# One hybrid encoder layer: head scales in one operation, edge columns on ScalarE, a split rotation and a new order of the mixer

## The chip, the cores and the metric

The kernel runs on one core of a Trainium2 chip. A core has five engines that run at the same time, each through its own list of instructions: PE (TensorE, matrix products into PSUM), DVE (VectorE), ACT (ScalarE), POOL (GpSimd) and SP (SyncE, which here only issues transfers). An engine takes its instructions strictly in the order of its list; one that has to wait for another engine or for a transfer holds up everything behind it. The metric is the time of one execution on the device in microseconds (us); smaller is better.

## The reference

One layer works on 512 positions of 1024 features, in single precision:

```python
x = x + 0.5 * swiglu(rms_norm(x, g1), w_gate1, w_up1, w_down1)
u = rms_norm(x, gm) @ w_in          # fourier 512 | q 8x64 | k 2x64 | v 2x64
a = fourier_mixer(u[:, :512])       # real part of a 2-D transform over positions and the
                                    # 128 channels of each of 4 groups, then fnet_w, fnet_b
q, k = rms_norm per head, then the axial rotation:
       [x1*cos - x2*sin, x1*sin + x2*cos] on each half of a head
b = softmax(q @ k.T / 8) @ v        # 8 query heads share 2 key heads
x = x + concat(a, b) @ w_out
x = x + 0.5 * swiglu(rms_norm(x, g2), w_gate2, w_up2, w_down2)
y = rms_norm(x, gf)
```

The feed-forward width is 2752. `rms_norm(x, g)` is x times (mean of squares + 1e-6) to the power -1/2 times g.

## The kernel before, in words

Activations lie transposed in SBUF: features (or head channels) on the 128 partitions, the 512 positions along the row. The program has three parts, one after the other: the first feed-forward block, the mixer (projection, Fourier branch, attention, output projection; roughly 345 to 495 us of the profiled span), and the second feed-forward block with the final norm. Only the mixer is touched here.

**Products in three passes.** PE multiplies in a format that is rounded. To keep single precision, every operand is held as a high part (a rounded copy) and a low part (the value less its high part), and `product` (L171 to L174) runs high by high (L172), high by low (L173) and low by high (L174). So each weight block and each intermediate needs two more operations before PE may use it: the high part, which ACT makes (or DVE for names in `HI_DVE`), and the low part, a subtraction (`lows`, L131) on DVE, or on POOL for names in `LOWS_POOL`. PE's first two passes can begin with the high parts of the weights alone; what each pass waits for is the part it reads.

**Who sets the order.** The mixer is written as some 600 small named steps. Each is recorded by `op(name)`, and the table `ORDER` lists the names in the order in which they are executed; each engine, SP's and POOL's queues of transfers too, gets its instructions in exactly this order. So one step placed earlier in the table is placed ahead of other steps on every engine that it uses.

The names: `wX.r/.h/.l` load a weight block and make its parts (X is k, q0 to q3, v, f0 to f3, fw, o0 to o7). `k.0` to `v.7` are the eight steps of each projection of keys, queries and values. Per query block q0 to q3, and for k, the rotation consists of `.sw` (ACT copies the projection times the gain), `.sd` (SP transfers that swap the halves into a second tile `sw_q`), `.rc` (DVE, times the cosines, into `rot_q`), `.rs` (DVE, L944: `sw_q` times the sines; L945: added to `rot_q`). Then `.ah/.al/.bh/.bl` make high and low parts of the two head sets in `qa` and `qb`. The scale of a head comes from squares (`.sq`, ACT), sums of them on PE (`.pq`), two small DVE operations (`.s0`, L962 and L963), a power on POOL (`.s1`, L968) and a factor on POOL (`.s2`, L972); the factors `rr` and `rq` are made from the norm of the mixer's input in step `n1.p` (L1397, L1398). Keys get their scale through `kw` (a broadcast copy), `kp` (PE transposes it) and `km`; `k0.0` to `k1.3` make their high and low parts in `ks`.

Attention works on 32 items `tbc` (query block t, key head b, block c of 128 queries): `s` (two matmuls of scores, L1230 and L1231), `m` (DVE: scale and row extreme, L1236), `e` (ACT: exponential, L1245), `x` (DVE: a transposition, L1254), `h` and `l` (parts, into `its`). `vr0.*` and `vr1.*` spread the values with transfers on POOL's queue, four each (L1062). `p0` to `p3` multiply probabilities with values; `o*.c/.a`, `z*.r/.w/.p` and `r*.m/.h/.l` add, divide by the sums and split the result. The Fourier branch: `f{h}{c}.0/.1` (PE, L1101), `.u` (ACT) or `.e` (DVE, L1122), `.h/.l`; `map*`; `d{g}0/1` (product over positions) with `.h/.l`; then `c{g}.c` and `c{g}.s` (the products with cosines and sines over the channels), `c{g}.q` (ACT copy), `c{g}.o` (DVE, into the tile `fo`: the two edge columns at L1207, two halves of 255 columns at L1211), `c{g}.h/.l`. The output projection is `y{d}.0` to `y{d}.7` (d is a block of 128 features), then `y{d}.x` (DVE, adds to x, L1337), `.h` (ACT) and `.l` (DVE, L203), which scale and split x for the next block, `.q` (ACT, square, L209) and `.a` (DVE, adds the squares in `acc`, L1350), whose sum gives the next norm (products `ss`, L231).

**Banks.** All products of the mixer share the eight PSUM banks. A step takes the bank that has been free the longest when the table reaches it (`bank_for`), and hands it back after its last reader (`read`). A product can therefore also wait for the engine that reads what was in its bank before.

## Time and profile before

| | |
|---|---|
| median of 3 runs | 833.85 us (832.57, 833.85, 833.99) |
| the profiled execution | 831.53 us |
| its span, first to last instruction | 829.7 us |
| outside the span | 1.8 us |
| mean granted TensorE clock | 0.999 |
| busy: PE, DVE, ACT, POOL | 818.9, 602.6, 458.7, 131.9 us |

The rows follow in the prediction. In rows of the timeline the first number is the start in us from the start of the span, the second the length, then engine, line, operation, what it writes and reads, and in brackets how long the engine was idle before it and who released it. The columns of a row by windows are: the stretch, its length, busy time (and count) of PE, of PE's weight loads, DVE, ACT and POOL, the granted clock, the share of the DMA engines, GB/s. Groups of instructions show engine, operation, out<-in, count, then busy us and mean ns of one, then idle time ahead of them and who ended it.

### The profile page before, as it was taken

How to read it: one execution, taken by the hardware profiler on the slowest of the kernel's cores; microseconds unless marked ns; L12 is line 12 of the kernel's file. 1: busy time of each engine (PE TensorE's matmuls, PEld its weight loads, DVE VectorE, ACT ScalarE, POOL GpSimd, SP SyncE). 2: the span in 40 equal slices, each digit the busy share in tenths (PEclk: the TensorE clock that was granted, in tenths of full speed). 3: DMA queues.
4: the chain of work that ended last, by engine and by line, in shares of the span. 5: the costliest groups of instructions: out<-in, count | busy, mean ns of one | idle time of the engine just before them, and what ended most of it. 6: DMA issues, size and time to landing. Idle time of an engine off the chain costs nothing.

```text
span 829.7 us, 14444 instructions
## 1 busy us (share of the span) xinstructions
PE 818.9 (99%) x5734; PEld 742.5 (89%) x5734; DVE 602.6 (73%) x939; ACT 458.7 (55%) x794; POOL 131.9 (16%) x138
## 2 busy tenths in 40 slices
PE   9999999999999999999989999999999999999997
PEld 6888998899989998889978878899988998899986
DVE  7987884578656857699998578878745884578562
ACT  7664663366434645577887257546623663266452
POOL 0121000000000000259794300200000000000001
PEclk9999999999999999999999999999999999999999
DMA  7787774567374514335350335877463774566122
GB/s 255 190 188 205 185 204 139 112 170 216 89 195 122 152 40 133 127 108 121 100 101 28 97 103 130 214 185 205 134 190 92 193 192 134 127 166 181 45 81 102
DMA packets 50724, 119.33 MB, mean 144 GB/s; under 512 B 5728, under 2 KB 14560, under 8 KB 50528
## 3 DMA queue, kind: packets, MB, share of 16 engines
q1 hardware_dynamic: 38128, 92.57, 34.1%
q0 software_dynamic: 12256, 25.57, 18.7%
q8 instruction: 45, 0.74, 0.4%
q10 hardware_dynamic: 272, 0.26, 0.1%
q14 instruction: 23, 0.19, 0.1%
HBM read 111.83 MB, written 2.10 MB: 137 GB/s over the span
## 4 chain that ended last, share of the span: by engine, by line
PE 95%; DVE 3%; issue 1%; POOLq 0%; POOL 0%; ACT 0%; DVEq 0%
PE r L449 23%; PE q L449 11%; PE dn L173 9%; PE dn L172 9%; PE dn L174 9%; PE p L449 6%; PE mix L172 3%; PE mix L174 3%; PE mix L173 3%; PE gu L787 3%; PE gu L172 2%; PE gu L174 2%; PE gu L173 2%; PE mix L1270 2%; PE mix L1101 1%; PE last L1475 1%
## 5 line engine op out<-in xcount | busy, mean ns | idle before, releaser
L449 PE MATMUL r<-rt,ring 128*128 128x256 f32 x1686 | 204.9, 277 | 0.0
L449 PEld LDWEIGHTS r<-rt,ring 128*128 128x128 f32 x1686 | 198.5, 188 | 0.9
L173 PE MATMUL dn<-at,ring 128*128 128x512 f32 x295 | 114.9, 389 | 0.0
L174 PE MATMUL dn<-at,ring 128*128 128x512 f32 x295 | 114.9, 389 | 0.0
L172 PE MATMUL dn<-at,ring 128*128 128x512 f32 x295 | 114.9, 389 | 0.0
L449 PE MATMUL q<-rt,ring 128*128 128x256 f32 x840 | 106.6, 276 | 0.0
L394 ACT CAST ring<-s 128x1024 fp32r<-128x1024 f32 x70 | 73.4, 1049 | 58.2 <-DVE s L414 51.4
L601 DVE SCALAR_TENSOR_TENSOR gx<-dn,gx 128x512 f32<-128x512 f32 x61 | 42.1, 691 | 80.5 <-PE dn L174 80.5
L449 PEld LDWEIGHTS q<-rt,ring 128*128 128x128 f32 x840 | 100.4, 188 | 0.0
L366 POOL DMA_DIRECT2D s<-in_wgu x35 | 30.1, 860 | 424.3 <-DMA s<-in_wgu 177.5
L131 DVE TENSOR_TENSOR ring<-s,ring 128x1024 fp32r<-128x1024 f32 x70 | 85.3, 1219 | 0.6 <-ACT ring L394 0.6
L164 ACT CAST ring<-raw_dn 128x768 fp32r<-128x768 f32 (+2 forms) x48 | 40.8, 853 | 75.4 <-PE dn L173 70.5
L174 PEld LDWEIGHTS dn<-at,ring 128*128 128x128 f32 x295 | 55.4, 188 | 11.5
L173 PEld LDWEIGHTS dn<-at,ring 128*128 128x128 f32 x295 | 55.4, 188 | 11.0
L172 PEld LDWEIGHTS dn<-at,ring 128*128 128x128 f32 x295 | 55.4, 188 | 11.0
L449 PE MATMUL p<-rt,ring 128*128 128x256 f32 x420 | 53.3, 276 | 0.0
L131 DVE TENSOR_TENSOR ring<-raw_dn,ring 128x768 fp32r<-128x768 f32 (+2 forms) x48 | 46.7, 977 | 7.0 <-ACT ring L164 6.9
L449 PEld LDWEIGHTS p<-rt,ring 128*128 128x128 f32 x420 | 50.2, 188 | 0.0
L131 DVE TENSOR_TENSOR ring<-raw_g,ring 128x1024 fp32r<-128x1024 f32 x36 | 43.8, 1217 | 0.0
L131 DVE TENSOR_TENSOR at<-u,at 128x512 fp32r<-128x512 f32 x35 | 24.2, 693 | 20.2 <-ACT at L504 20.2
L492 DVE TENSOR_TENSOR u<-g,u 128x512 f32<-128x512 f32 x35 | 24.0, 687 | 19.8 <-ACT u L489 19.8
L131 POOL TENSOR_TENSOR its<-x,its 128x512 fp32r<-128x512 f32 x26 | 36.0, 1406 | 7.0 <-ACT its L1256 6.6
(332 smaller groups left out, 1551.7 us busy)
## 6 DMA issues: line engine op xcount, KB each, us to landing
raw_g<-in_wgu SPq DMA_DIRECT2D x36, 512.0 KB, 4.1
s<-in_wgu SPq DMA_DIRECT2D x70, 256.0 KB, 4.3
s<-in_wgu POOLq DMA_DIRECT2D x35, 512.0 KB, 5.7
raw_dn<-in_wd SPq DMA_DIRECT2D x44, 384.0 KB, 4.0
raw_u<-in_wgu SPq DMA_DIRECT2D x35, 256.0 KB, 4.0
raw_gu<-in_wgu SPq DMA_DIRECT2D x11, 512.0 KB, 3.5
raw_o<-in_wo SPq DMA_DIRECT2D x8, 512.0 KB, 3.8
raw_dn<-in_wd SPq DMA_DIRECT2D x5, 448.0 KB, 4.2
```

The lines of the kernel that those rows point to most:

```text
L131: (by or nc.vector).tensor_tensor(out=lo, in0=src, in1=asf(hi), op=ALU.subtract)
L164: nc.scalar.copy(hi[:, :n, :], raw[:, :n, :])
L172: nc.tensor.matmul(ps, whi, mhi, start=first, stop=False)
L173: nc.tensor.matmul(ps, whi, mlo, start=False, stop=False)
L174: nc.tensor.matmul(ps, wlo, mhi, start=False, stop=last)
L366: nc.gpsimd.dma_start(out=blocks(t), in_=up, accum_op=ALU.add)
L394: nc.scalar.copy(ts[0], src)
L449: nc.tensor.matmul(ps[:, c], a[:, ks], b[:, i, c], start=first and i == 0 and o == 0, stop=i == KH - 1 and o == 2, skip_group_check=not fi ...
L492: nc.vector.tensor_tensor(out=self["u"], in0=self["g"], in1=self["u"], op=ALU.mult)
L601: nc.vector.scalar_tensor_tensor(out=x[d][:, t], in0=ps[:, t], scalar=0.5, in1=x[d][:, t], op0=ALU.mult, op1=ALU.add)
L787: nc.tensor.matmul(pss[c], w[:, k % 2, c], m[k], start=k == 0 and m is hh and w is hi, stop=k == KD - 1 and w is lo,)
L1270: nc.tensor.matmul(sets[st][a][:, : 8 * 32], vrep[rows, j], its[rows, o, :, 32 * j : 32 * j + 32], start=j == 0 and o == 0, stop=j == 15 a ...
```

## The change

- **Head scales (`.s0`, `.s1`).** One DVE operation in place of two: sums/64 plus `em`, where `em` is EPS times the input norm's mean of squares. The power on POOL stays, `.s2` and the factors `rr` and `rq` go: the norm of the mixer's input cancels in a normalized head but for its EPS term. The factor -1/8 goes into the gain of the queries (`qkg[:, 0:1]`). Both preparations stand on POOL ahead of the power of the input's norm in `n1.p`.
- **`kw`** is a copy on ACT, before on DVE.
- **Edge columns.** New steps `c{g}.t` on ACT (Identity with a bias) in place of the DVE operation at L1207.
- **The rotation's addition** is a step of its own, `.ra`. For the names in the new table `ADDS_DMA`, which holds q2, it is a transfer on POOL's queue that adds `sw_q` (128 rows of 512) to `rot_q` in place of the DVE operation.
- **`k1.1` and `k1.2`** are transfers on POOL's queue (64 rows of 512) that copy the part that another step made, in place of a DVE subtraction and an ACT copy.
- **Two tables** of who makes which part: 33 names in place of 34 in `LOWS_POOL`; `HI_DVE` has 300, f0, o3, o4, wq3 in place of 203, o3, o6, o7, wq1, wq2.
- **`ORDER`** is new. The number of matmuls stays the same.

```diff
 LOWS_POOL = """
-000 001 003 010 011 012 013 100 101 102 103 110 111 113 200 201 202 203 211 212 213 300 301 303 311 312 f0 fw o0 o1
-o2 o5 o6 o7
+000 002 010 011 012 013 100 101 103 110 111 113 200 201 202 203 212 213 300 301 302 303 310 311 313 f3 o0 o1 o2 o4
+o5 o6 wq3
+ADDS_DMA = """
+q2
 HI_DVE = """
-203 o3 o6 o7 wq1 wq2
+300 f0 o3 o4 wq3
...
 ORDER = """
-wk.r wq0.r wv.r cos wk.h wk.l wq0.h k.0 k.1 k.2 k.3 k.4 wv.h k.5 wq0.l k.6 wq1.r k.7 k.sq q0.0 wq1.h n1.c q0.1 wq3.r
+wk.r wq0.r wv.r cos wk.h wk.l wq0.h k.0 k.1 k.2 k.3 k.4 wv.h k.5 wq0.l k.6 wq1.r k.7 k.sq q0.0 wq1.h n1.c k.pq q0.1
...
             @op(f"{name}.rs")
             def _():
+                sw = swaps[name]
+                nc.vector.tensor_tensor(out=sw, in0=sw, in1=sin, op=ALU.mult)
+
+            @op(f"{name}.ra")
+            def _():
                 r, sw = rots[name], swaps[name]
-                nc.vector.tensor_tensor(out=sw, in0=sw, in1=sin, op=ALU.mult)
-                nc.vector.tensor_tensor(out=r, in0=r, in1=sw, op=ALU.add)
+                if name in ADDS_DMA:
+                    nc.gpsimd.dma_start(out=r, in_=sw, accum_op=ALU.add)
+                else:
+                    nc.vector.tensor_tensor(out=r, in0=r, in1=sw, op=ALU.add)
...
             @op(f"{name}.s0")
             def _():
                 pq = banks[f"pq{name}"][:, 0:8].rearrange("p (c t) -> p c t", t=2)
-                nc.vector.tensor_tensor(out=pq, in0=pq, in1=rr.unsqueeze(2).to_broadcast([P, 4, 2]), op=ALU.mult)
-                nc.vector.tensor_scalar(out=v, in0=pq, scalar1=1.0 / HD, scalar2=EPS, op0=ALU.mult, op1=ALU.add)
+                nc.vector.scalar_tensor_tensor(
+                    out=v, in0=pq, scalar=1.0 / HD, in1=em.unsqueeze(2).to_broadcast([P, 4, 2]), op0=ALU.mult, op1=ALU.add
+                )
                 read(f"pq{name}")
...
-            @op(f"{name}.s2")
-            def _():
-                nc.gpsimd.tensor_tensor(out=v, in0=v, in1=factor.unsqueeze(2).to_broadcast([P, 4, 2]), op=ALU.mult)
...
             @op("kw")
             def _():
-                nc.vector.tensor_copy(kw, sc[0].unsqueeze(3).to_broadcast([P, 4, 2, HD]))
+                nc.scalar.copy(kw, sc[0].unsqueeze(3).to_broadcast([P, 4, 2, HD]))
...
+                if v:
+                    op("k1.1")(lambda own=own, oth=oth, h1=h1, h2=h2: nc.gpsimd.dma_start(out=h1[oth], in_=h2[own]))
+                    op("k1.2")(lambda own=own, oth=oth, h1=h1, h2=h2: nc.gpsimd.dma_start(out=h2[oth], in_=h1[own]))
+                    op("k1.3")(lambda own=own, h1=h1, h2=h2: lows(h2[own], rots["k"][own], h1[own]))
+                    continue
...
+            @op(f"c{g}.t")
+            def _():
+                fos[g, 1] = o = tp.tile([P, S], F32, tag="g", name=f"fo{g}")
+                nc.scalar.activation(
+                    o[:, 0:257:256], banks[f"pc{g}"][:, 0:257:256], AF.Identity, bias=fb[:, g : g + 1]
+                )
...
-                nc.vector.tensor_scalar(
-                    out=o[:, 0:257:256], in0=pc[:, 0:257:256], scalar1=b, scalar2=None, op0=ALU.add
-                )
...
         @op("n1.p")
         def _():
+            nc.gpsimd.tensor_scalar(out=em, in0=n1.ms, scalar1=EPS, scalar2=None, op0=ALU.mult)
+            nc.gpsimd.tensor_scalar(out=qkg[:, 0:1], in0=qkg[:, 0:1], scalar1=-scale, scalar2=None, op0=ALU.mult)
             n1.power(0, 4)
-            nc.gpsimd.tensor_tensor(out=rr, in0=n1.r, in1=n1.r, op=ALU.mult)
-            nc.gpsimd.tensor_scalar(out=rq, in0=n1.r, scalar1=-scale, scalar2=None, op0=ALU.mult)
```

What the new order does is shown at three places. A line number moves by 4 to 16 between the two programs (L131 is L135 after, L1350 is L1366).

The first place is the end of the mixer on DVE, before: `gx<-mix` is `y7.x`, the two operations on `raw_gu` belong to the next block's weights, `ring<-gx` are `y5.l` and `y7.l`, and `acc` with `sq_5`, `sq_7`, `sq_6` are the additions `y5.a`, `y7.a`, `y6.a`.

```order
L1337 TENSOR_TENSOR gx<-mix_3406,gx 128x512
L203 SCALAR_TENSOR_TENSOR ring<-gx,ring 128x512
L1350 TENSOR_TENSOR acc_5277<-acc_5277,sq_5_0_5366 128x512
L131 TENSOR_TENSOR ring<-raw_gu_1_5410,ring 128x1024
L131 TENSOR_TENSOR at_5405<-raw_gu_42_5414,at_5405 128x1024
L203 SCALAR_TENSOR_TENSOR ring<-gx,ring 128x512
L1350 TENSOR_TENSOR acc_5277<-acc_5277,sq_7_0_5381 128x512
L1350 TENSOR_TENSOR acc_5277<-acc_5277,sq_6_0_5384 128x512
```

The same place on DVE after:

```order
L1353 TENSOR_TENSOR gx<-mix_3406,gx 128x512
L207 SCALAR_TENSOR_TENSOR ring<-gx,ring 128x512
L135 TENSOR_TENSOR ring<-raw_gu_1_5399,ring 128x1024
L135 TENSOR_TENSOR at_5394<-raw_gu_42_5403,at_5394 128x1024
L207 SCALAR_TENSOR_TENSOR ring<-gx,ring 128x512
L1366 TENSOR_TENSOR acc_5218<-acc_5218,sq_7_0_5374 128x512
```

The additions of `y5.a` and `y6.a` have moved ahead of `y7.x`.

The second place is the channel stage of the Fourier branch on DVE, before: `oo` is `r1.m`, `el` is `c1.l`, the two L1236 are `m312` and `m212`, then `x313`, `d31.l` (the low part that `c3.s` reads) and `c2.o`.

```order
L1315 TENSOR_TENSOR oo_4188<-mix_3405,oo_4188 128x512
L131 TENSOR_TENSOR el_3423<-fo_4695,eh_3419 128x512
L1236 TENSOR_SCALAR mix_3403,mx_4733<-mix_3403,sc_3438 128x512
L1236 TENSOR_SCALAR mix_3409,mx_4735<-mix_3409,sc_3437 128x512
L1254 STREAM_TRANSPOSE x_4739<-e_4623 128x512
L131 TENSOR_TENSOR ring<-mix_3407,ring 128x255
L1207 TENSOR_SCALAR fo_4751<-mix_3404,fb 128x2
L1211 SCALAR_TENSOR_TENSOR fo_4751<-mix_3404,fb,fq_4723 128x255 x2
```

After, from `c0.l` (`el`) over `c1.o` and `d31.l` (128x255) to `m312`, `m313`, `x212` and `d30.l` (128x257):

```order
L135 TENSOR_TENSOR el_3422<-fo_4604,eh_3418 128x512
L1227 SCALAR_TENSOR_TENSOR fo_4655<-mix_3409,fb,fq_4682 128x255 x2
L135 TENSOR_TENSOR ring<-mix_3408,ring 128x255
L1252 TENSOR_SCALAR mix_3402,mx_4700<-mix_3402,sc_3438 128x512
L1252 TENSOR_SCALAR mix_3407,mx_4710<-mix_3407,sc_3438 128x512
L1270 STREAM_TRANSPOSE x_4721<-e_4693 128x512
L135 TENSOR_TENSOR ring<-mix_3406,ring 128x257
```

`c1.o` and `d31.l` have come ahead of the two `m`, `r1.m` is earlier still, and the last low part in the row is that of `d30`; `c3.s` and `c2.c` on PE stand behind these.

The third place is DVE around the rotation of q2, after: L948 on `sw_q_3704` is `q2.rs`; `rot_q_3815` and `sw_q_3781` are q3's; `qa_3430` is `q2.al`.

```order
L948 TENSOR_TENSOR sw_q_3704<-sw_q_3704,early 128x512
L135 TENSOR_TENSOR ring<-raw_f_3694,ring 128x1024
L940 TENSOR_TENSOR rot_q_3815<-early 128x512
L1252 TENSOR_SCALAR mix_3406,mx_3817<-mix_3406,sc_3436 128x512
L1252 TENSOR_SCALAR mix_3405,mx_3833<-mix_3405,sc_3436 128x512
L135 TENSOR_TENSOR its<-x_3774,its 128x512
L135 TENSOR_TENSOR its<-x_3787,its 128x512
L948 TENSOR_TENSOR sw_q_3781<-sw_q_3781,early 128x512
L973 SCALAR_TENSOR_TENSOR sc_3438<-mix_3404,em 128x8
L1270 STREAM_TRANSPOSE x_3868<-e_3842 128x512
L135 TENSOR_TENSOR qa_3430<-rot_q_3741,qa_3430 64x512
```

Before, the product with the sines and the addition stood together and `q2.al` came six operations later:

```order
L944 TENSOR_TENSOR sw_q_3719<-sw_q_3719,early 128x512
L945 TENSOR_TENSOR rot_q_3778<-rot_q_3778,sw_q_3719 128x512
L1236 TENSOR_SCALAR mix_3408,mx_3811<-mix_3408,sc_3436 128x512
L1254 STREAM_TRANSPOSE x_3815<-e_3767 128x512
L962 TENSOR_TENSOR mix_3402<-mix_3402,rr 128x8
L963 TENSOR_SCALAR sc_3437<-mix_3402 128x8
L936 TENSOR_TENSOR rot_q_3820<-early 128x512
L131 TENSOR_TENSOR qa_3430<-rot_q_3778,qa_3430 64x512
```

The addition of q2 has left DVE; it stands on POOL's queue, after, behind four transfers of values:

```order
L1075 DMA vrep<-its 32x4x128 x4
L954 DMA rot_q_3741<-sw_q_3704 128x512
L135 TENSOR_TENSOR its<-x_3699,its 128x512
L1075 DMA vrep<-its 32x4x128 x4
L980 TENSOR_TENSOR sc_3437<-sc_3437,mhalf 128x8
```

More of the change, by code (lines that the diff above doesn't have):

```diff
@@ L71 @@
-z0.r d00 z0.w o10.c o11.c z1.r h112 d00.h o2.l x113 d01 x110 map0.l m013 d01.h o10.a o11.a d00.l d01.l d10 o1.l h012
-s213 d10.h l112 d11 e013 d10.l m213 h113 s313 x011 s010 h110 c0.s d11.h c0.q h011 s111 vr1.0 m010 vr1.1 d21 l012
-l110 c0.c m313 e010 m111 e313 d20 d11.l d21.h l113 c0.o x010 o4.r d30 d20.h d20.l c0.h d21.l c0.l c1.s c1.c l011
-c2.s h010 vr1.3 z0.p d30.h x013 vr1.2 c1.q e111 o0.r d30.l c2.c s212 c1.o d31 s312 x111 z1.w h013 z1.p c1.h r0.m
-e213 y2.0 c2.q d31.h l010 h111 s311 o0.h l013 c1.l m312 m212 s310 x313 l111 d31.l e212 c3.s y2.1 c2.o r1.m e312 c3.q
@@ new lines @@
+q3.sw q3.sd x003 s100 f2.h q2.rs q3.sq h002 f03.0 vr0.2 h001 e103 f1.l q3.rc m100 f01.0 h003 q2.ra m101 l001 q3.pq
+l003 q3.rs e100 q3.s0 f02.0 h102 q2.ah l002 q2.pq vr0.3 x100 q2.al q2.s0 q2.bh q3.ra f02.1 l102 q2.s1 f00.0 f00.1
+fw.r s203 s202 f2.l q3.s1 q3.ah x103 q3.al f03.1 s200 e101 f3.h f00.u m202 s201 h100 x101 s302 q3.bh z0.r f01.1 m203
+h103 f02.e e202 m200 h101 f3.l m201 e203 s300 x202 m300 f01.u e200 l100 f02.h l103 o1.r e201 z0.w fw.h f03.e x203
+o2.r q3.bl l101 f03.h f11.0 f02.l s303 f11.1 e300 f11.u m302 x200 p0 x300 e302 h200 f03.l s301 pos fw.l h300 f10.0
@@ new lines @@
+e111 c0.t z1.p l013 d10.h d21 r1.m x111 d10.l l113 s010 d21.h m010 e213 d20 d31 c1.s h111 d21.l c1.c e010 d20.h c1.t
+c0.o c0.h d31.h l111 x010 d20.l x011 s212 h010 o0.r d30 m212 c1.q c0.l s313 c1.o c2.s h011 e212 s312 d30.h r1.h
+d31.l m312 vr1.0 vr1.3 m313 y2.0 c1.h c2.c c2.q x212 s311 c2.t d30.l e312 e313 c2.o l011 c3.s l010 x213 c3.c c1.l
+c3.q m311 s310 o0.h c3.t p2 x312 r0.h y2.1 e311 s210 c2.h c3.o c3.h m310 e310 y1.0 r0.l h212 y1.1 h312 c2.l s211
+z2.r c3.l x313 m210 o0.l o20.c h213 l212 l312 h313 l213 x311 m211 x310 e210 y2.2 h311 y1.2 y0.0 y0.1 e211 o20.a x211
```

52 lines of the change are left out of this document (24 added, 28 removed).

## The prediction

> **What bounds the kernel now.** I read the page first (busy shares, the chain that ended last), then PE's waits, then the timeline where they lie, and last the price groups of the mixer. From the page:
>
> ```profile
> span 829.7 us, 14444 instructions
> PE 818.9 (99%) x5734; PEld 742.5 (89%) x5734; DVE 602.6 (73%) x939; ACT 458.7 (55%) x794; POOL 131.9 (16%) x138
> PE 95%; DVE 3%; issue 1%; POOLq 0%; POOL 0%; ACT 0%; DVEq 0%
> ```
>
> PE is busy for 818.9 of 829.7 us and the chain runs on it for 95%. The change leaves every matmul as it is, so it can only win PE's waits inside the mixer, or add some. These are PE's waits by line, the mixer's among them:
>
> ```profile
> PE mix L172 <- DVE ring L131: 1.6, 1, 1.6
> ...
> PE mix L173 <- DVE ring L131: 0.8, 1, 0.8
> PE ss L231 <- DVE acc L1350: 0.8, 1, 0.8
> PE mix L172 <- ACT e L1245: 0.4, 1, 0.4
> PE mix L172 <- DVE oo L1315: 0.3, 1, 0.3
> ```
>
> With 0.24 at a `gu` product (quoted below) they come to 1.65 + 0.81 + 0.76 + 0.39 + 0.26 + 0.24 = 4.1 us. That is the whole prize: 831.5 - 4.1 = 827.4 on the basis of the profiled execution. Four lie in the channel stage (3.1 us), two at the mixer's end (1.0 us). By windows, the first half of the mixer's attention is:
>
> ```profile
> 380.00:430.00 50.00, 48.80 (x555) 45.59 (x554) 49.30 (x117) 41.48 (x103) 43.42 (x44) 1.00 0.47 112
> ```
>
> DVE is busy for 49.30 of 50 us there and PE for 48.80, with the clock at 1.00. DVE is as full as PE, yet PE waits for it only at the very end of this stretch: work for DVE is stored ahead of its need. A lighter DVE is worth something only where PE stands waiting; a badly placed step costs at once.
>
> **End of the mixer.** The timeline there (start, length, engine):
>
> ```profile
> 489.89 0.69 DVE L1337 TENSOR_TENSOR gx<-mix,gx 128x512 f32<-128x512 f32 x1
> ...
> 491.15 0.68 DVE L1350 TENSOR_TENSOR acc<-acc,sq 128x512 f32<-128x512 f32 x1
> 491.75 1.22 DVE L131 TENSOR_TENSOR ring<-raw_gu,ring 128x1024 fp32r<-128x1024 f32 x1
> ...
> 493.97 0.39 PE L174 MATMUL gu<-ring 128*128 128x512 f32 x1
> 494.02 0.75 DVE L203 SCALAR_TENSOR_TENSOR ring<-gx,ring 128x512 fp32r<-128x512 f32 x1
> 494.20 0.39 PE L172 MATMUL gu<-ring 128*128 128x512 f32 x1
> 494.68 1.48 DVE L1350 TENSOR_TENSOR acc<-acc,sq 128x512 f32<-128x512 f32 x2
> 494.82 0.50 PE L173 MATMUL gu<-ring 128*128 128x512 f32 x1 [0.24 <-DVE ring L203]
> ...
> 495.16 0.40 PE L174 MATMUL gu<-ring 128*128 128x512 f32 x1
> 496.31 1.02 PE L231 MATMUL ss<-ones,acc 128*128 128x2 f32 x8 [0.76 <-DVE acc L1350]
> ```
>
> Undisturbed products start 0.23 us apart (493.97, 494.20). The one at 494.82 starts 0.62 after its forerunner and the sums 1.15 after theirs, so the two stops cost 0.39 + 0.92 = 1.31 us. From `y7.x` to `y7.l` DVE now runs `y5.l`, `y5.a`, two weight lows and `y7.l`; `y5.a` takes 491.75 - 491.15 = 0.60 there. The new order has `y5.a` and `y6.a` before `y7.x`: `y7.l` comes 0.60 earlier, of which 0.39 is needed, and `acc` is ready two additions earlier (1.2 to 1.35) where 1.31 is needed. DVE has room for them earlier, since it waits for the products of `y7`. Term: **-1.3 us**, with a slack of only 0.2 at the first and of about nothing at the second; bounds -1.3 and 0.
>
> **Channel stage.** The timeline around its longest wait:
>
> ```profile
> 431.04 0.65 DVE L1315 TENSOR_TENSOR oo<-mix,oo 128x512 f32<-128x512 f32 x1
> ...
> 431.09 4.21 POOL L131 TENSOR_TENSOR its<-x,its 128x512 fp32r<-128x512 f32 x3
> 431.62 1.33 DVE L131 TENSOR_TENSOR el<-fo,eh 128x512 fp32r<-128x512 f32 x1
> ...
> 432.55 0.39 PE L1230 MATMUL mix<-ks,qb 128*128 128x512 f32 x1
> ...
> 432.87 0.74 DVE L1236 TENSOR_SCALAR_CACHE_REDUCE mix<-mix,sc 128x512 f32<-128x512 f32 x1
> ...
> 433.01 0.39 PE L1230 MATMUL mix<-ks,qb 128*128 128x512 f32 x1
> ...
> 434.84 0.37 DVE L131 TENSOR_TENSOR ring<-mix,ring 128x255 fp32r<-128x255 f32 x1
> ...
> 435.27 0.39 PE L172 MATMUL mix<-ring 128*128 128x256 f32 x1 [1.65 <-DVE ring L131]
> ```
>
> `c3.s` starts when `d31.l` (434.84 + 0.37) is done. Ahead of `d31.l` on DVE stand `c1.l`, two `m` (0.74 each) and a transposition. After, the same product waits for `d30.l`, and from `c0.l` DVE has to run, start to start, `c0.l` 0.6, `c1.o` two halves 0.8, `d31.l` 0.33, `m312` and `m313` 0.67 each and `x212` 0.63 to `d30.l` 0.31, in all some 3.4 to 3.7 us; PE between has `y2.0` (three passes), `c2.c` and one pair of scores (0.46: 432.55 to 433.01), about 1.5. So the wait is about 1.9, partly at `c2.c`, which needs its bank, mostly at `c3.s`. `y2.0` waits for `c0.l` for 0.8 more by the same laying of rows, and `p2` for its banks for 0.3. The three waits of before that went (0.81, 0.39, 0.26) and 1.65 at `c3.s`, 3.1 in all, are against 1.9 + 0.8 + 0.3 = 3.0. Term: **-0.1 us**; bounds -1.5, if half of the new waits do not come (the edge columns are gone from each `c{g}.o`), and +1.3, if two lows of this stage are lengthened as `el` is here.
>
> **The other parts.** Groups of the mixer's window (engine, what is written and read, count, busy us, mean ns, idle time ahead):
>
> ```profile
> L945 DVE TENSOR_TENSOR rot_q<-rot_q,sw_q 128x512 f32<-128x512 f32 x4 | 2.8, 692 | 0.1
> L131 DVE TENSOR_TENSOR ks<-rot_k,ks 64x512 fp32r<-64x512 f32 x4 | 2.7, 684 | 0.5 <-ACT ks L1021 0.4
> L962 DVE TENSOR_TENSOR mix<-mix,rr 128x8 f32<-128x8 f32 x5 | 0.9, 172 | 1.2 <-POOL rr L1397 1.2
> L1207 DVE TENSOR_SCALAR fo<-mix,fb 128x2 f32<-128x2 f32 x4 | 0.8, 199 | 0.0
> L1004 DVE COPY kw<-sc 128x512 f32<-128x512 f32 x1 | 0.4, 422 | 0.0
> L1304 ACT COPY zw<-za 128x512 f32<-128x512 f32 x4 | 2.5, 615 | 0.0
> L1062 POOL DMA_DIRECT2D vrep<-its x16 | 8.9, 569 | 1.9 <-DVE its L131 1.9
> ```
>
> Transfers on POOL's queue (KB each, median us from issue to landing):
>
> ```profile
> vrep<-its POOLq DMA_DIRECT2D x16, 64.0 KB, 2.0
> late<-in_chan POOLq DMA_DIRECT2D x1, 256.0 KB, 4.6
> late<-in_odd POOLq DMA_DIRECT2D x1, 129.0 KB, 6.3
> s<-in_wgu POOLq DMA_DIRECT2D x35, 512.0 KB, 5.7
> ```
>
> *Head scales:* five operations of 0.17 leave DVE (0.9 us); they and POOL's factors were no one's last release on PE, so the price on the path is 0. *`kw`:* 0.42 leaves DVE, and ACT gets a broadcast copy like `zw`, 0.62; the transposition `kp` that reads it lies among the projections, where PE has other products and no wait: 0, bounds ±0.3. *Edge columns:* 0.8 off DVE, counted in the channel stage; ACT gets four short operations, ahead of the DVE step that follows, bounded by 0.2 (DVE's own row) and 0.62 (the longest ACT row here) each. *`k1.1`, `k1.2`:* 0.68 off DVE and one copy off ACT against two transfers of 128 KB. Their readers are the scores of the second key head, which come more than 20 us later, so even 5.7 us hides: 0. On POOL they add two issues of about 0.57 each, where POOL's own operations are down by seven. In `n1.p` the power comes some 0.4 us later behind two small operations; its readers are not among those that release PE: 0. *The two tables:* the same kinds of operations (a part of a weight or of an item) change engines, about as many each way: 0, bounds ±0.5. In all DVE is lighter by 0.9 + 0.4 + 0.8 + 0.7 + 0.7 = 3.5 us.
>
> *`q2.ra` by a transfer.* Between `q2.rs` and `q2.al` DVE runs ten operations: a low of 1.22, `q3.rc`, two `m`, two lows, `q3.rs`, a scale, a transposition, start to start about 5.6 us. Of these the queue of POOL takes some 0.9 (the four issues of 0.57 ahead are partly done by then) and ACT's `q2.ah` 0.62 (as `zw`). So the transfer may take about **4.0 us** from its issue before DVE and, with the stored work gone, PE notices; beyond that it costs nearly 1:1. It moves 256 KB within SBUF and adds. No row shows that kind. 64 KB within SBUF (`vrep`) take 2.0, 512 KB that add from memory (`s`) 5.7; in a straight line between, 256 KB take 2.0 + 3.7 x 192/448 = 3.6 us, hidden by 0.4. The 256 KB from memory take 4.6: +0.6. I take 3.6, since it stays inside SBUF like the row of 2.0, and keep 2.0 (0) and 6.3, the slowest row, issued behind others of its queue (+2.3), as ends.
>
> [...]
>
> *Score stage.* With `q2` and `q3` side by side, DVE runs `q3.ra`, two lows, a weight low, two transpositions, `q3.al`, two `m` and `f02.e` between `q2.al` and the release of the bank that `s300` takes: some 6.5 us start to start. PE stands 1.2 us behind `q2.al` when it starts `s203`, and then has five pairs of scores (0.46 each, above) and two Fourier halves to `s300`. A half is twelve products, 0.34 for three by their rows:
>
> ```profile
> 389.24 0.28 PE L1101 MATMUL mix<-ring 128*128 128x256 f32 x1
> 389.58 0.28 PE L1101 MATMUL mix<-ring 128*128 128x256 f32 x1
> ```
>
> So PE needs 5 x 0.46 + 2 x 1.36 = 5.0 us: a new wait of about 6.5 - 1.2 - 5.0 = 0.3. In the same way a Fourier product near 401 us waits about 0.4 for the bank that `e303` on ACT frees. Before, PE did not wait in this stretch. Term: **+0.7 us**, bounds 0 and +1.8 (each of both twice, or 0.4 more each).
>
> **Sum.** -1.3 - 0.1 + 0.7 + 0 = -0.7 us: 831.5 becomes 830.8 on the profiled execution's own basis (span 829.7 and 1.8 outside). That execution is 2.3 below the median of the runs, 833.85, so the forecast for the median is **833.1 us**.
>
> **Rivals.** (A) *No new waits:* the 2 us or so that DVE is lighter when it reaches the score stage swallow the 0.7, and half of the channel stage's 3.0 goes too. For it: DVE is the releaser of almost every wait. Against it: PE's waits depend on the order in front of one product, not on DVE's sum. Then -1.3 - 0.1 - 1.5 = -2.9: 831.0. (B) *The addition of q2 is late,* the slower side: it costs from 4.0 us after its issue and turns the forecast into a loss from 4.7. At 5.7 it costs 1.7 (834.8); at 6.3, 2.3, and if its issue slips by one low of POOL (4.21 / 3 = 1.4 in the row at 431.09) besides, 3.7: 835.4 to 836.8. For it: four transfers of values stand ahead in the same queue, and no row of this size or more on this queue is under 4.6. Against it: those of the kind that stays in SBUF are at 2.0. (C) *Collisions of DVE with POOL:* at 431.62 a low of two inputs took 1.33 while POOL ran lows from 431.09, against 0.68 for a low of the same length (`ks`). Two such on the way to `c3.s` cost 1.3: 834.4. (D) *The mixer's end does not close,* since the slack is 0.0 to 0.2: +0.9 on the forecast, 834.0, near no change.
>
> [...]
>
> **Chances.** The forecast with (D), 832.2 to 834.5: 0.48; (A) 0.18; (B) 0.20; (C) 0.14. A measurement of this kernel tells from no change what is beyond about 0.2%, 1.7 us: faster is under 832.2, slower over 835.5. Faster: nearly all of (A) and a seventh of the forecast, 0.24. Slower: 0.12 of (B), a third of (C) and 0.03 for what I have not seen, 0.20. The rest, 0.56, is within. The range that leaves out 2 in 10 reaches from (A) into the upper half of (B): 831.0 to 836.3; the forecast's own is 832.2 to 834.5.
>
> **What will show it.** The end: no wait of a `gu` product for `ring` L207 and none of `ss` for `acc` L1366 before 500 us. Channel stage: a wait of 1.5 to 2 us at a product `mix` with 256 columns that `ring` L135 ends, one of about 0.8 for `c0.l`. Score stage: two waits of 0.3 to 0.4 between 388 and 403 us. The transfer `rot_q<-sw_q`: under 4.0 us from issue to landing, and ACT with no long idle time ahead of `qa<-rot_q`; over it, the forecast is wrong by what is over. DVE's busy time in the mixer falls by about 3.5 us. If PE's waits in the mixer sum to less than 2 us, (A) was right; if the time is longer with these waits as said, the cause lies outside them.

## The result

| | before | after |
|---|---|---|
| median of 6 executions | 833.85 us (831.68 to 834.62) | 829.72 us (829.37 to 830.40) |
| the profiled execution | 831.53 us | 829.37 us |
| its span | 829.7 us | 827.5 us |

The ratio of the times is 0.994, with a 95% interval of 0.9915 to 0.9966: the change is faster by 4.1 us in the median. The forecast was 833.1, range 831.0 to 836.3, no measurable change likeliest. Two things stand out. The two profiled executions differ by 2.2 us, the medians by 4.1; and the executions of before lie 2.9 us apart, those of after 1.0.

The page of after, its lines on the span, busy time and the chain:

```profile
span 827.5 us, 14438 instructions
PE 818.3 (99%) x5734; PEld 742.0 (90%) x5734; DVE 598.7 (72%) x927; ACT 460.4 (56%) x799; POOL 131.4 (16%) x135
PE 93%; DVE 4%; issue 1%; POOL 1%; ACT 0%; DMA 0%; POOLq 0%; SPq 0%; DVEq 0%; ACTq 0%
```

DVE is busy for 3.9 us less. PE's waits of after, all that are left:

```profile
PE mix L177 <- DVE ring L135: 1.4, 1, 1.4
PE busy L730 <- DVE halves L760: 1.0, 1, 1.0
PE mix L1246 <- DVE fe L1135: 0.7, 1, 0.7
```

In the mixer 2.1 us of waits are left of 4.1. By place:

**End of the mixer.** The timeline of after shows `y7.x` at 489.03, then `y5.l`, two weight lows, `y7.l` and one addition; the sums start with no wait:

```profile
489.03 0.68 DVE L1353 TENSOR_TENSOR gx<-mix,gx 128x512 f32<-128x512 f32 x1
489.63 0.73 DVE L207 SCALAR_TENSOR_TENSOR ring<-gx,ring 128x512 fp32r<-128x512 f32 x1
...
492.56 0.74 DVE L207 SCALAR_TENSOR_TENSOR ring<-gx,ring 128x512 fp32r<-128x512 f32 x1
493.22 0.68 DVE L1366 TENSOR_TENSOR acc<-acc,sq 128x512 f32<-128x512 f32 x1
...
494.15 0.95 PE L235 MATMUL ss<-ones,acc 128*128 128x2 f32 x8
```

(In the order of before shown further up, the first `ring<-gx` behind `y7.x` is `y6.l`, not `y5.l`; the count of operations is as said there.)

**Channel stage.** The row by windows of the 13 us around it, of before and then of after:

```profile
424.00:437.00 13.00, 9.90 (x64) 8.14 (x64) 13.00 (x33) 11.21 (x28) 12.99 (x15) 1.00 0.27 41
```

```profile
424.00:437.00 13.00, 11.43 (x112) 9.53 (x114) 13.00 (x33) 12.00 (x33) 11.59 (x15) 1.00 0.28 43
```

PE stands idle for 13.00 - 9.90 = 3.1 us before and 13.00 - 11.43 = 1.6 after, while DVE is full in both. The timeline of after:

```profile
430.17 0.69 DVE L135 TENSOR_TENSOR el<-fo,eh 128x512 fp32r<-128x512 f32 x1
430.39 0.39 PE L176 MATMUL mix<-eh,more 128*128 128x512 f32 x1
...
430.92 0.50 PE L177 MATMUL mix<-el,more 128*128 128x512 f32 x1
...
433.86 0.39 DVE L135 TENSOR_TENSOR ring<-mix,ring 128x257 fp32r<-128x257 f32 x1
...
434.30 0.39 PE L177 MATMUL mix<-ring 128*128 128x256 f32 x1 [1.39 <-DVE ring L135]
```

`c3.s` waits 1.39 us for `d30.l`, as the prediction's laying of rows had it. `y2.0`, which was to wait 0.8 for `c0.l`, starts its second pass 0.53 behind the first (0.3 lost), and the small waits at `c2.c` and `p2` are not there.

**Score stage.** `s300` waits 0.74 us for `f02.e` (the row of 0.7 above). It is the one new wait, over twice the 0.3 forecast; the second one, for an exponential, did not come.

**The addition of q2** took 3.7 us from issue to landing; ACT stood 1.6 us for it, which reached no product: PE has no wait there. The transfer, and the group of ACT that reads its result, of after:

```profile
rot_q<-sw_q POOLq DMA_DIRECT2D x1, 256.0 KB, 3.7
```

```profile
L990 ACT CAST qa<-rot_q 64x512 fp32r<-64x512 f32 x4 | 2.5, 616 | 2.8 <-DMA rot_q<-sw_q 1.6 <-DVE rot_q L956 1.3
```

From profile to profile the sum closes: -1.3 (end) - 1.5 (channel stage) + 0.7 (score stage) = -2.1, against 831.53 - 829.37 = 2.16. Ahead of the mixer the two profiles run alike: the product that starts at 297.91 us before starts at 297.89 after. The experiments are about the rest: which parts bring this, and where the other 2 us of the medians come from.

### The profile page after: what moved, and what is told of

Its sections match the earlier page's. It is cut to its first block, busy times and chain, and to the rows that moved or that the text cites. A ratio compares the mean times of both kernels' runs of the same rounds, so it can differ in the third digit from the quotient of the medians.

```text
span 827.5 us, 14438 instructions
## 1 busy us (share of the span) xinstructions
PE 818.3 (99%) x5734; PEld 742.0 (90%) x5734; DVE 598.7 (72%) x927; ACT 460.4 (56%) x799; POOL 131.4 (16%) x135
## 4 chain that ended last, share of the span: by engine, by line
PE 93%; DVE 4%; issue 1%; POOL 1%; ACT 0%; DMA 0%; POOLq 0%; SPq 0%; DVEq 0%; ACTq 0%
PE r L453 23%; PE q L453 12%; PE dn L178 9%; PE dn L176 9%; PE dn L177 9%; PE p L453 6%; PE mix L176 3%; PE mix L177 3%; PE mix L178 3%; PE gu L791 3%; PE gu L176 3%; PE gu L177 3%; PE gu L178 3%; PE mix L1286 2%; PE last L1491 1%
## 5 line engine op out<-in xcount | busy, mean ns | idle before, releaser
L135 DVE TENSOR_TENSOR ring<-s,ring 128x1024 fp32r<-128x1024 f32 x70 | 85.3, 1218 | 0.6 <-ACT ring L398 0.6
L135 DVE TENSOR_TENSOR ring<-raw_dn,ring 128x768 fp32r<-128x768 f32 (+2 forms) x48 | 46.7, 977 | 7.1 <-ACT ring L168 7.0
L135 DVE TENSOR_TENSOR ring<-raw_g,ring 128x1024 fp32r<-128x1024 f32 x36 | 43.8, 1216 | 0.0
L135 DVE TENSOR_TENSOR at<-u,at 128x512 fp32r<-128x512 f32 x35 | 24.2, 692 | 20.3 <-ACT at L508 20.2
L398 ACT CAST ring<-raw_g 128x1024 fp32r<-128x1024 f32 x35 | 36.8, 1051 | 0.0
```

Source lines behind the costliest of these rows:

```text
L135: (by or nc.vector).tensor_tensor(out=lo, in0=src, in1=asf(hi), op=ALU.subtract)
L398: nc.scalar.copy(ts[0], src)
```

## The experiments

Medians are of all executions of a kernel in its group of runs; the kernel before had medians of 833.76 to 834.41 in the five groups.

| kernel | median us (lowest to highest) | ratio to before, 95% interval |
|---|---|---|
| changed kernel | 829.72 (829.37 to 830.40) | 0.994 (0.9915 to 0.9966) |
| after_end_undone | 830.96 (830.05 to 831.42) | 0.996 (0.9946 to 0.9975) |
| after_q2_dve | 830.41 (829.71 to 831.64) | 0.9963 (0.9949 to 0.9977) |
| after_dve_back | 830.88 (830.24 to 831.47) | 0.9963 (0.9951 to 0.9975) |
| after_swap_back | 833.43 (832.65 to 835.26) | 1.0002 (0.999 to 1.0014) |
| order_tables | 834.62 (834.12 to 836.64) | 1.001 (0.9996 to 1.0024) |
| order_alone | 844.78 (844.63 to 845.60) | 1.0129 (1.0112 to 1.0146) |
| ops_alone | 839.26 (837.80 to 840.23) | 1.006 (1.0045 to 1.0075) |
| ahead | 830.75 (830.41 to 830.85) | 0.9961 (0.9949 to 0.9974) |
| ahead_f | 831.13 (830.55 to 832.37) | 0.9967 (0.9953 to 0.9982) |
| ahead_d | 829.62 (829.20 to 830.67) | 0.996 (0.9945 to 0.9975) |
| before_again | 834.48 (831.62 to 836.77) | 1.0002 (0.9986 to 1.0018) |
| before_swap | 833.56 (831.82 to 836.49) | 0.9994 (0.9978 to 1.001) |
| before_l003 | 835.91 (832.10 to 837.97) | 1.0018 (0.9999 to 1.0037) |
| before_clean | 834.26 (832.06 to 836.32) | 1.0005 (0.9991 to 1.0019) |
| before_tail | 831.31 (830.17 to 834.92) | 0.9965 (0.9946 to 0.9984) |
| before_tail_swap | 832.45 (830.27 to 834.17) | 0.9978 (0.996 to 0.9996) |

### Order, tables and operations apart

*ops_alone*: the new operations in the old order, with the old tables:

```diff
 ORDER = """
-... k.s1 ... k.s2 ... k.rs ... c0.o ...
+... k.s1 ... k.rs k.ra ... c0.t c0.o ...
```

> The new operations (head scales in one operation, kw and edge columns on ACT, q2's addition and two key copies as transfers) in the old order, with the old tables of who makes which part. Theory that the order brings the gain: 833.5 to 834.5, both waits at the mixer's end stay (1.0 us), c3.s waits 1.2 to 1.6 us, and q2's addition, which the old order reads six DVE operations later, comes late, so that q2.al and with it PE lose 0 to 2 us. Rival, that the lighter DVE brings it: 831 to 832, with at most 1.5 us of waits in the channel stage.

839.26, 5 us slower than before. Both theories missed it. Its waits on PE, the largest of the mixer:

```profile
PE mix L175 <- DVE ring L134: 1.7, 1, 1.7
PE mix L1017 <- ACT kw L1011: 1.3, 1, 1.3
PE mix L1245 <- DVE qa L134: 1.2, 1, 1.2
PE mix L1245 <- ACT e L1260: 1.1, 2, 0.7
...
PE mix L1245 <- DVE sc L972: 0.9, 1, 0.9
```

The channel stage's 1.7 is as it was although the edge columns are off DVE. The copy for the key scales, which the prediction moved to ACT at no price, stops PE for 1.3 us, since in the old order ACT has other work ahead of it. The addition of q2 holds up its readers: ACT's `q2.ah` stands 2.61 us for it.

*order_alone*: the kernel before with the new `ORDER`, all old operations and the old tables:

```diff
 ORDER = """
-... k.s0 ... k.s1 k.rc ... k.ra ... c0.c c0.q ... c0.t ...
+... k.s0 ... k.s1 k.s2 k.rc ... k.rs ... c0.c c0.q ...
```

(lines with - as the changed kernel has it; `.rs` does both operations at the place of `.ra`).

> The new order with all the old operations and the old tables (the rotation's addition at the place of its new step, edge columns with c.o, factors behind the powers). Theory that the order brings the gain: 829.5 to 831, no waits at the mixer's end, c3.s waits 1.5 to 2 us (edge columns of c1 and c2 stand ahead of d30.l), s300 waits 0.7 to 1.5 us. Rival, that the lighter DVE brings it: 832 to 834, with 3 us or more of waits in the channel stage.

844.78, 11 us slower: neither theory. The timeline shows one DVE operation of 4.94 us in place of 0.69, with two lows of POOL in its time:

```profile
373.54 2.70 POOL L1062 DMA_DIRECT2D vrep<-its  x5
375.47 4.94 DVE L131 TENSOR_TENSOR qb<-rot_q,qb 64x512 fp32r<-64x512 f32 x1 [0.24 <-ACT qb L990]
376.24 1.31 POOL L131 TENSOR_TENSOR its<-x,its 128x512 fp32r<-128x512 f32 x1
377.49 2.36 POOL L131 TENSOR_TENSOR ring<-raw_f,ring 128x1024 fp32r<-128x1024 f32 x1
```

It began 0.77 us before the first of the two lows, while POOL was still issuing transfers (until 376.24); what held it in that time is not shown. PE itself waits most for two other things:

```profile
PE mix L1270 <- DVE its L131: 3.4, 1, 3.4
PE mix L1103 <- POOL ring L131: 2.3, 1, 2.3
```

The 2.3 is a Fourier product at 379.90 that waits for POOL's low of f0, the third POOL row above. The 3.4 is a product with the probabilities at 462.37 that waits for low parts of items. Behind the first the granted clock is 0.66 over 5 us (380 to 385), behind the second 0.74 and 0.92 over 5 us each (460 to 470), a loss of 1.7 us each time. order_tables has neither wait. So the old tables cost PE these two waits and two falls of the clock here, 9.1 us together.

*order_tables*: the same with the two new tables.

```diff
 LOWS_POOL = """
-000 001 003 ... 311 312 f0 fw o0 o1 o2 o5 o6 o7
+000 002 010 ... 311 313 f3 o0 o1 o2 o4 o5 o6 wq3
 HI_DVE = """
-203 o3 o6 o7 wq1 wq2
+300 f0 o3 o4 wq3
```

> The new order with the new tables of who makes which part, and all the old operations. Theory that order and tables belong together and the operations add about 3.5 us of room on DVE: 831 to 835, so most of the 15 us between the new order with the old tables and the changed kernel is the tables'; waits behind q1.al and qb (the 4.94 us operation at 375.5 that stood behind two lows of POOL) are gone. Rival, that the new order needs the lighter DVE: 838 to 845, with waits of PE for DVE between 370 and 400 us.

834.62: the tables give back 10.2 us, the new operations the last 4.9 (834.62 to 829.72, in two groups of runs). Neither the whole order nor the operations bring anything alone (the tables alone were not tried): each part is worth what it is only inside the order that was made for it.

*after_swap_back*: one name of the tables back, in the changed kernel: POOL makes the low of f0, DVE that of wq3.

```diff
-... f3 o0 o1 o2 o4 o5 o6 wq3
+... f3 o0 o1 o2 o4 o5 o6 f0
```

> The changed kernel with f0's low on POOL and wq3's on DVE, as before. Theory of the collision: 0 to 3 us slower than 829.7 with a wider spread, as far as the two lows meet in the new order too. If they don't meet there, within 0.5 us of 829.7.

833.43: 3.7 us slower, over the 0 to 3 expected, and not by a meeting of the two lows. POOL's low of f0 (2.37 us) comes too late:

```profile
377.49 2.37 POOL L135 TENSOR_TENSOR ring<-raw_f,ring 128x1024 fp32r<-128x1024 f32 x1
...
379.91 0.38 PE L1116 MATMUL mix<-ring 128*128 128x256 f32 x1 [2.87 <-POOL ring L135]
```

and the clock that TensorE is granted falls behind the wait (row by windows; the clock is the third number from the end):

```profile
380.00:385.00 5.00, 5.00 (x31) 5.00 (x31) 5.00 (x8) 1.72 (x6) 5.00 (x8) 0.66 0.94 220
```

0.66 over 5 us costs another 1.7 us.

### Single parts of the changed kernel

*after_end_undone*: `y5.a` and `y6.a` back behind `y7.x`.

```diff
-... y6.q y7.7 y5.a y6.l y6.a y7.x y5.l y7.h y7.q y7.l y7.a
+... y7.7 y6.l y7.x y5.l y7.h y7.q y5.a y6.q y7.l y7.a y6.a
```

> The changed kernel with the additions of y5 and y6 to the sum of squares back behind y7.x, in the places of the kernel before. By the term for the mixer's end: +1.3 us over 829.7, so 831.0, with a wait of a gu product for y7.l of 0.2 and of the sums for acc of 0.8. If the end's waits are covered in another way by the new order, no change: 829.7.

830.96, +1.24, with a wait of the sums for `acc` of 0.8 in its profile. The term of the mixer's end stands as far as its waits go.

*after_q2_dve*: q2's addition on DVE.

```diff
 ADDS_DMA = """
-q2
 """.split()
```

> The changed kernel with q2's addition on DVE again. By the prediction's steps the transfer is hidden (3.7 us from issue to landing) and frees 0.69 us of DVE ahead of f02.e, for which s300 waits 0.74: so 0.7 us slower, 830.4, with s300 waiting 1.4. Rival, that the transfer itself delays ACT (1.59 us idle before q2.ah) and so costs more than it frees: no change or faster, 828.5 to 829.7.

830.41, +0.69, the first theory's size, but not by its path: `s300` waits 0.7 as in the changed kernel; what is new is a wait of 0.3 for a high part on ACT, and in this profile the addition took 1.30 us behind a low of POOL.

*after_dve_back*: `kw` on DVE, and the edge columns on DVE as the first operation of `c{g}.o`.

```diff
-                nc.scalar.copy(kw, sc[0]...)
+                nc.vector.tensor_copy(kw, sc[0]...)
-            @op(f"c{g}.t") ...
+                nc.vector.tensor_scalar(out=o[:, 0:257:256], in0=pc[:, 0:257:256], scalar1=b, ...)
```

> The changed kernel with kw and the edge columns on DVE again. c1.o stands ahead of d30.l, for which c3.s waits 1.39: by the lighter DVE 0.2 to 0.4 us more there, and kw at 352 us costs nothing: 830.0. Rival, that the changed kernel's order leans on this room elsewhere: over 831.

830.88, +1.16. `c3.s` waits 1.4 as in the changed kernel; new are 0.3 at `y2.0` for `c0.l` and 0.2 for `c1.o`, of the kind that had been forecast for the changed kernel. In the profile, which is 1.10 slower, they are the smaller part. Laid beside the profile of the changed kernel product by product, PE is 0.54 us behind at 388 us already (the start of the span, see below), 0.83 at 430 and 1.19 at 440. So the edge columns bring about 0.4 us of the 1.4 that were not expected of the channel stage. What brings the other 1.0 no run here shows.

*ahead*: `f02.e` directly behind `m202`, `d30.l` directly behind `d31.l`; *ahead_f* moves the first alone, *ahead_d* moves `d30.l` alone, behind `m312`. Of *ahead*:

```diff
-... f00.u m202 s201 h100 x101 s302 q3.bh z0.r f01.1 m203 h103 f02.e ...
+... f00.u m202 f02.e s201 h100 x101 s302 q3.bh z0.r f01.1 m203 h103 ...
-... d31.l m312 vr1.0 vr1.3 m313 y2.0 c1.h c2.c c2.q x212 s311 c2.t d30.l ...
+... d31.l d30.l m312 vr1.0 vr1.3 m313 y2.0 c1.h c2.c c2.q x212 s311 c2.t ...
```

> The changed kernel with two steps moved earlier: f02.e, which frees the bank of s300, directly behind m202, and d30.l, for which c3.s waits 1.39 us, directly behind d31.l. If these two waits are what is left, PE's waits in the mixer fall from 2.1 to under 0.7 us and the time from 829.7 to 828.0 to 828.6. If the steps that are now later (x101, m203, m312, m313) make others wait, 829 to 830.

> The changed kernel with f02.e directly behind m202. The combined try (with d30.l too) was 1.0 us slower, with new waits of 1.6 us for an exponential at a Fourier product and 0.9 us at p2. If f02.e brought the first of them: s300's wait of 0.74 goes, the 1.6 stays, 830.5. If not: 829.0.

> The changed kernel with d30.l directly behind m312, one step of 0.7 us and one transposition earlier. If the late step is all: c3.s waits 0.1 instead of 1.39, 828.5 to 829. If m313 and x212, now later, hold up p2: p2 waits for an exponential by 0.3 to 0.9, 829.2 to 829.7.

Both together: 830.75, 1.0 us slower, with new waits of 1.6 us (a Fourier product for an exponential) and 0.9 (`p2` for an exponential); a further 0.9 of `gu` products for a weight high lies in the first 9 us of the span, ahead of the mixer. *ahead_f* has the 1.6 and 831.13: the step was right where it stood. *ahead_d* takes the 1.39 away and gets 0.5 at `p2`: 829.62 (ratio to before 0.996), level with the changed kernel. No version was found that is clearly faster.

### The spread of the kernel before

*before_again*, *before_p2*, *before_p3*: the kernel before, unchanged.

> The kernel before once more, unchanged. Ratio 1.000 within 0.2%. Theory of sensitivity: its executions lie about 3 us apart, because lengthened DVE operations fall in front of products that already wait, and this profile shows 1 to 3 us more of PE's waits in the mixer than the 4.1 us of the first profile, when its time is near 833.9. Rival: the 2 us by which the profiled execution was under the median lie outside the mixer (feed-forward blocks, or outside the span); then PE's waits in the mixer are 4.1 us again and the windows before 345 or after 500 us are longer.

> The kernel before, a third profiled execution. Theory: if its time is over 833, its mixer has one wait of PE that the first profile (831.5) lacks, for a DVE or ACT operation lengthened behind POOL; if the wait is over 2 us, the granted clock falls behind it (0.66 over 5 us after waits of 2.3 and 2.9 us in other runs of this case). If it is under 832.5, its waits are those of the first profile, 4.1 us in the mixer.

> The kernel before, a fourth profiled execution; as for the third.

before_again was profiled at 835.13, before_p2 at 833.67, before_p3 at 831.66. The fast one has the waits of the first profile. The first two lose part of their time outside the mixer, as the rival had it. These are the products in the first us of the span, of the first profile, before_p2 and before_again:

```profile
4.68 3.56 PE L787 MATMUL gu<-ring 128*128 128x512 f32 x14
4.82 3.50 PE L787 MATMUL gu<-ring 128*128 128x512 f32 x11
4.59 3.67 PE L787 MATMUL gu<-ring 128*128 128x512 f32 x10
```

The first products run at half their later pace (0.43 us from start to start against 0.23), until 5 us in the first profile and until 6.9 in before_again. From there to the mixer every product comes 0.77 us (before_p2) and 0.95 us (before_again) later than in the first profile. In the 20 profiles of this case the first 10 us put PE at most 1.1 us behind the first profile.

In the mixer the two have one more meeting each of DVE with POOL. In before_again:

```profile
364.36 2.74 POOL L131 TENSOR_TENSOR ring<-raw_f,ring 128x1024 fp32r<-128x1024 f32 x1 [1.50 <-ACT ring L874]
364.75 3.42 DVE L131 TENSOR_TENSOR more<-raw_wq,more 128x1024 fp32r<-128x1024 f32 x1
...
368.23 0.50 PE L174 MATMUL mix<-ring,more 128*128 128x512 f32 x1 [1.70 <-DVE more L131]
```

POOL's low of f0 began 0.39 us before DVE's low of wq3, which ended 1.07 us behind it. In the first profile DVE was first, by 0.72 us (362.68 against 363.40), and its low took 1.22. In before_p2 it is 0.07 us by which POOL is ahead of the addition of q2:

```profile
378.51 1.34 POOL L131 TENSOR_TENSOR its<-x,its 128x512 fp32r<-128x512 f32 x1
378.58 1.83 DVE L945 TENSOR_TENSOR rot_q<-rot_q,sw_q 128x512 f32<-128x512 f32 x1
```

In the first profile the addition was 0.22 us ahead of POOL's low (377.55 against 377.77) and took 0.69. The changed kernel has the one addition as a transfer and the two lows on each other's engine. In the rows above, where POOL was first, DVE's operations took 3.42 us in place of 1.22 and 1.83 in place of 0.69, and ended 1.07 and 0.56 us behind POOL's. In order_alone DVE's operation of 4.94 us ended 0.56 behind the second of the two lows of POOL (380.41 against 379.85), though it had begun before the first.

*before_swap* exchanges the lows of f0 and wq3 (`f0` in `LOWS_POOL` becomes `wq3`); *before_l003* moves POOL's low of item 003, the one of 378.51, behind `q2.s1`; *before_clean* does both:

```diff
 LOWS_POOL = """
-... 311 312 f0 fw o0 o1 o2 o5 o6 o7
+... 311 312 wq3 fw o0 o1 o2 o5 o6 o7
 ORDER = """
-... q2.al l003 m102 ... e102 q2.s1 s200 ...
+... q2.al m102 ... e102 q2.s1 l003 s200 ...
```

> The kernel before with one exchange: POOL makes the low part of wq3 and DVE that of f0 (the changed kernel has both so). Theory of the collision: in the second profile of before DVE's low of wq3 started at 364.75, 0.39 after POOL's low of f0, and took 3.42 us instead of 1.22, and PE waited 1.70 for it; in the first profile DVE was first and nothing happened. Without the meeting the slow half of the executions goes: median 831.5 to 832.5, spread from lowest to highest under 2.5 us. Rival, that the spread comes from elsewhere: median 833.5 to 834.5 and a spread of 4 us or more.

> The kernel before with one step moved: POOL's low of item 003, which in the slower of two profiles starts 0.07 us before DVE's addition for q2, goes behind q2.s1 on POOL. Theory of the second meeting: the cluster of executions at 833.2 to 835 goes to 831.5 to 832.5, but for those that have the first meeting; median 832 to 832.5. Rival: median 833.5 to 834.3 as before.

> The kernel before with both meetings taken away: the low of item 003 behind q2.s1, and the lows of f0 and wq3 exchanged between DVE and POOL. Theory that both make the spread: median 831.5 to 832.2, spread under 1.5 us, so about 2 us of the change's 4.1 are these meetings. Rival: median over 833.

833.56, 835.91 and 834.26: none is faster than before, so the meetings alone do not make the 2 us. before_l003 and before_clean have a wait of 0.6 to 0.7 us for an exponential, at the score product where before_again (0.5) and before_p2 (0.7) have one and the first profile has none; its cause is open. But the profile of before_l003 shows another thing, the clock behind the waits at the mixer's end:

```profile
498.00:500.00 2.00, 2.00 (x11) 1.70 (x11) 1.18 (x3) 1.77 (x3) 0.71 (x1) 0.85 0.41 147
500.00:502.00 2.00, 2.00 (x6) 1.56 (x5) 1.23 (x1) 0.14 (x1) 0.33 (x1) 0.50 0.74 244
502.00:504.00 2.00, 2.00 (x8) 1.59 (x8) 0.00 (x0) 0.00 (x0) 0.00 (x0) 0.80 0.73 221
```

PE is busy throughout, at 0.85, 0.50 and 0.80 of its clock: 0.3 + 1.0 + 0.4 = 1.7 us lost. In the profiles of 831.5, 831.7, 833.7 and 835.1 us the clock stays at 1.00 there. The mean clock of each execution shows how often this may be: of 132 executions of before in these groups, 54 have a mean clock of 0.997 or less, none of them under 833.6 us, median 835.0; 78 have 0.998 or more, 37 of them under 832.8 and 40 over 833. So the clock is one cause of the spread and not the only one. (1.7 of 830 us are 0.002 of the mean. The count is rough, since the mean also holds the half clock behind PE's last product: 0.73 and 0.50 in the two us from 827 of before.) All six of the changed kernel are at 0.998 or 0.999.

*before_tail*: the kernel before up to `r3.l`, then the output projection in the order of the changed kernel, with what belongs to o4:

```diff
 LOWS_POOL = """
-... f0 fw o0 o1 o2 o5 o6 o7
+... f0 fw o0 o1 o2 o5 o6 o4
 HI_DVE = """
-203 o3 o6 o7 wq1 wq2
+203 o3 o4 wq1 wq2
 ORDER = """
-... r3.l o3.r y2.7 y0.6 o3.h o3.l y0.7 ... y7.x y6.l y7.h y7.q y5.a y6.q y7.l y7.a y6.a
+... r3.l o3.r y2.7 o3.h y1.7 o5.h y0.6 ... y5.a y6.l y6.a y7.x y5.l y7.h y7.q y7.l y7.a
```

*before_tail_swap*: the lows of f0 and wq3 exchanged besides.

> The kernel before with the steps behind r3.l (output projection and norm) in the changed kernel's order, and o4's parts made where the changed kernel makes them. The waits at the mixer's end go: 1.3 us for every execution, so the fastest at 830.2 to 830.6 instead of 831.5. Theory that these waits set off the slower clock: besides, executions with a mean clock of 0.997 or less fall from 4 in 10 to under 2 in 10, median 830.5 to 831.8. Rival, that the channel stage sets it off: they stay at 4 in 10, median 832.3 to 833.0.

> As before_tail, with the lows of f0 and wq3 exchanged between DVE and POOL besides (first meeting gone, second left). Clock as in before_tail; by the meetings, one class of executions above 833 goes: median 830.3 to 831.8. Rival: the same as before_tail.

831.31 and 832.45, against 834.22 of before in the same group; the fastest executions are at 830.17 and 830.27, 1.4 below those of before (831.62). A mean clock of 0.997 or less is left in 1 of 12 and 0 of 12. In the same group 8 of 22 executions of before have one. So the output projection's order alone brings 2.9 us in the median of one kernel (interval 1.3 to 4.5) and 1.8 in that of the other (0.3 to 3.3): 1.3 of waits, which every execution has, and the rest in executions whose clock would have fallen. The executions over 833 that remain have a full clock; the one profiled (833.29) has the meeting of the two lows, with DVE's low at 3.43 us. Exchanging them did not lower the median further, against the theory of that meeting. From before_tail to the changed kernel 1.6 us remain. By the profiles the channel and score stages make 0.8 of it; that the missing meetings make the rest is not shown.

Not every execution with these waits loses the clock: none of the six of after_end_undone, which has a wait there too, fell under 0.998. Shorter rows give an estimate of why. Those of before_l003 around the fall:

```profile
499.00:499.50 0.50, 0.50 (x3) 0.41 (x3) 0.18 (x2) 0.41 (x1) 0.21 (x1) 0.89 0.26 107
499.50:502.50 3.00, 3.00 (x8) 2.31 (x8) 1.23 (x1) 0.64 (x1) 0.83 (x1) 0.50 0.61 187
502.50:503.00 0.50, 0.50 (x3) 0.36 (x3) 0.00 (x0) 0.00 (x0) 0.00 (x0) 0.70 0.50 106
```

The clock is at 0.50 for 0.11 + 3.00 + 0.30 = 3.41 us, and the same reading gives 3.41 us in after_swap_back. In before_l003 the next fall, behind PE's last product, comes 327.68 us after the clock has risen again, which is 96 times 3.413 (in after_swap_back 443.73, 130 times). In before and in after the traces have one rise, near the start, and one fall, behind PE's last product, 822.61 us apart in both: 241 times 3.413. So in these four traces the clock changes on a grid of 3.413 us. Where the grid lies differs from execution to execution: the rise comes 4.86 us from the start of the span in before, 4.01 in after.

An estimate from the 20 kept traces: lay this grid through each, and add up for each stretch of it the time in which PE ran no product, or only the eight small ones of the sums. Ahead of the four falls inside a span it is 2.16 us (before_l003), 2.38 and 3.38 (order_alone) and 2.75 (after_swap_back). No stretch with 2.06 or less is followed by a fall. At the mixer's end of before this time is 2.4 us if one stretch holds all of it, and it is over 2.1 for a third of the positions that the grid can have; in after_end_undone it is 2.16 at best, in before_tail 0.9. A third is near 54 of 132, and none of six and 1 of 24 with the new end fit too. The estimate rests on four falls, and no run moved the grid on purpose; what the clock answers to is not shown.

## Why the prediction was right or wrong

- **End of the mixer, -1.3:** right in its waits (both gone; +1.24 when undone). Mis-sized in the median: with the output projection's order alone before moved by -2.9 and -1.8, in two kernels. The clock behind those waits was not thought of, since the first profile has 1.00 there.
- **Channel stage, -0.1:** wrong; it measured -1.5 from profile to profile. The waits of 1.9 at `c2.c` and `c3.s` came as 1.4, those at `y2.0` (0.8) and `p2` (0.3) as 0.3 in all. The laying of rows for `y2.0` failed: it left DVE 0.5 us later at `c0.l` than it was. The prediction had room on DVE from the edge columns only as an end of the bounds and as rival (A). after_dve_back gives it about 0.4 us of the 1.4 missed; the rest stays open.
- **Score stage, +0.7:** right in sum by luck: one wait of 0.74, over twice its forecast, in place of two of 0.3 and 0.4.
- **The addition of q2:** right: 3.7 us against 3.6 forecast, the limit 4.0. It is hidden from PE, and worth 0.7 by after_q2_dve, though not at `s300`, where that theory had it. Rival (B) fell.
- **The tables, 0 ± 0.5, and `kw`, 0:** the prices hold only inside the new order. One name put back costs 3.7, all of them 10 (with the old operations), `kw` on ACT in the old order a wait of 1.3.
- **From one profile to the median:** this step failed, and it put the range wrong. It said that the profiled execution was 2.3 below the median and carried this over to the changed kernel as a constant. It was no constant. Part of before's executions lose up to about 1 us at the start of the span, 1.7 when the clock falls behind the mixer's end, and more where DVE meets POOL otherwise than in the first profile. The changed kernel's profile lies only 0.35 under its median (829.37, 829.72). That the new end of the mixer takes the falls away is shown by before_tail; that the missing meetings bring the rest is not shown. With the waits as they came (-2.2), the same step would have given 831.7, and the measured 829.7 is 2 us below it.
- **The rivals:** (A) was half right, for the channel stage; (C) is real, but it was a cost of the kernel before, not of the changed one, which has two such meetings less; without them before was no faster; (D) did not happen.

## What to carry to other kernels

Before a change is priced against one profiled execution, ask how far the executions of the same kernel lie apart and why: a wait may cost more in other executions than in the one that was profiled, and a change that removes it removes the spread too. A price of nothing for an operation moved to another engine belongs to one order; operations, order and the tables of who does what have to be tried together. Two engines that come close in time can make a race: DVE's addition took 0.69 us in the first profile, 0.22 ahead of POOL's low, and 1.83 in before_p2, 0.07 behind it.

## What the runs showed of the hardware that was not expected

- The granted clock of TensorE fell to 0.50 for 3.41 us with PE busy, right behind waits that sum to 1.0 us and eight small products (before_l003), and as long behind a wait of 2.87 (after_swap_back); behind one of 1.70 (before_again) it stayed at 1.00.
- A subtraction on DVE of 0.69 us took 4.94 with two operations of POOL, 1.31 and 2.36 us, one after the other in its time (order_alone).
- The first products of the span run at half pace, 0.43 us apart, for a time that differs between executions of the same kernel (until 5 us in the first profile, until 6.9 in before_again).
